# A two-layer decoder trunk in fp32 on one core: the MLPs' weights are prepared in a new order, five plain pairs instead of four, and plain tiles take their low halves from accumulating transfers

## The chip, the core and the metric

The kernel runs on one core of a Trainium2 chip. The metric is device time in microseconds (us); the engines are TensorE (PE; its weight loads are listed apart as PEld), VectorE (DVE), ScalarE (ACT), GpSimd (POOL) and SyncE (SP). SP and POOL only issue transfers here, apart from a few set-up instructions.

## The reference

One sequence of 512 tokens, width 1024, two layers. Each layer adds a mixer (layer 0: causal pooling and a convolution module; layer 1: latent attention with 16 heads), a cross-attention into 256 memory tokens, and a gated MLP with a causal convolution of three taps on the gate. A final RMSNorm follows. Everything is fp32.

```python
def conv_ffn(h, w_up, conv_w, conv_b, w_down):          # D_FF = 2816
    a, g = jnp.split(h @ w_up, 2, axis=-1)
    g = causal_dwconv(g, conv_w) + conv_b
    return (jax.nn.silu(g) * a) @ w_down

for l in range(DEPTH):                                   # DEPTH = 2
    x = x + (pool_conv_mixer if l % 2 == 0 else mla_attention)(rmsnorm(x, norm_mix_g[l]), ...)
    x = x + memory_cross_attention(rmsnorm(x, norm_xa_g[l]), rmsnorm(mem, norm_mem_g[l]), ...)
    x = x + conv_ffn(rmsnorm(x, norm_ffn_g[l]), ffn_w_up[l], ffn_conv_w[l], ffn_conv_b[l], ffn_w_down[l])
return rmsnorm(x, final_norm_g)
```

## The kernel before

**Number format.** Activations lie transposed: 128 channels by 512 tokens (`T`). Each operand of a matmul is split into a high half (a cast) and a low half (the rest), and a product is three matmuls, high by high, high by low, low by high (`mm3`, lines 173 to 175). Activations are split by an ACT cast and a DVE subtraction (lines 212 and 213). Weights come as tiles of 128 by 1024 (`wr`, one SP transfer of 512 KB, line 150, four buffers) and are split by `load_w` in the same way (lines 167 and 168) into `wh` and `wl`, three buffers each. `low_by_dma` (lines 160 and 161) makes the low half without DVE: ACT writes −1 times the tile, and a POOL transfer adds the tile from memory to it.

**The MLP** (`ffn`) works on 22 pairs of column blocks, a gate tile and an other tile, 128 columns each.

- The first four pairs (`PLAIN_PAIRS`) are *plain*: for each of the two tiles eight `mm3` of 512 columns into one PSUM bank `lin`, with weights from `load_w`. DVE multiplies the result by the row scale `rb`, `convolved` makes the gate `c` on ACT and DVE, and the product is split into `fh` and `fl`.
- Meanwhile `Operands.fill` builds the operands of the other 18 pairs on DVE and ACT, `OPERAND_STEPS` steps per plain tile: names `b…` and `t…`, from scaled activations `u`.
- The other 18 pairs are *paired*: a bilinear scheme forms both tiles by seven products (`a11`, `s1`, `s2`, `a12`, `s3`, `s4`, `a22`) of four `mm3` of 256 columns, in three banks `xyz`. `q` and `e` are copies of partial results; the bank of `a11` is used again by `s2`, so `q` must be copied first (line 684). The weight operands of the seven products come from four pieces per pair, `Weights.piece(0)` to `piece(3)`: the gate tile (split by `low_by_dma` into two buffers `wh1`, `wl1` of its own), the first sums, the second sums, and half of the other tile (the last three split by ACT and DVE, lines 559 and 560, in `wh` and `wl`). `need` releases pieces from a list by numbers, with `LEAD = 2`.
- `down()` is a generator that puts one `mm3` of 512 columns of the down projection behind each of the seven products. Its weights are tiles `dr` of 128 by 512 (256 KB, SP, line 638), one for each of eight output blocks and each of four groups of four pairs, split into `dwh` and `dwl`; the tile after the present one is fetched and split when the present one has done its first `mm3`. The fifth group (six pairs) follows as plain products, or in the last layer in `finale` (bank `fin`, weight halves `dh` and `dl`, lines 735 and 736).

**What sets the order.** A scheduler places the instructions of each engine in program order, moved forward by `tc.high_priority(offset=…)` (`AHEAD = 40` in `load_w`). Each engine then works its queue strictly in order, and so do the two queues that issue transfers, SP and POOL. A pool of 55 slots of 128 by 512 (`slot`) holds nearly all intermediate tiles, `dr` and the halves of activations among them.

In the latent attention, `kv` (the cross-attention's keys and values, kept in memory) is fetched and split by `split_kept` after the last head, and then follow the output projection and the cross-attention.

Of the kernel before, what the change touches and what calls it, by code (L numbers as in the profile page):

```python
# [19 lines left out]
P = 128  # L20
T = 512
# [39 lines left out]
RB_K = 6  # L61
LATE = (1, 4, 1, 3, 1, 4, 1)
FFN_GROUPS = (4, 4, 4, 4, 6)
PLAIN_PAIRS = 4
OPERAND_STEPS = 5
LEAD = 2
HALF = T // 2
KH = KD // 2

# [36 lines left out]
def kernel(ctx: ExitStack, tc: tile.TileContext, a):  # L106
# [46 lines left out]
    def parts():  # L153
        hi = wp.tile([P, WCOLS], F32R, tag="wh", name=uid("wh"), bufs=3)
        lo = wp.tile([P, WCOLS], F32R, tag="wl", name=uid("wl"), bufs=3)
        return hi, lo

    def low_by_dma(lo, raw, src):
# [232 lines left out]
        sp.dma_start(t, d)  # L391
        return t

    def split_kept(kv):
        kt, vt = kv
        return ([split_sb(fetch(t), "k", (P, 2, MEM)) for t in kt],
                [[split_sb(fetch(t), "v") for t in row] for row in vt])

    def split_kv(kv):
        kt, vt = kv  # L400
# [142 lines left out]
    class Weights:  # L543
# [16 lines left out]
            vec.tensor_tensor(lo[:, :n], raw, f(hi[:, :n]), ALU.subtract)  # L560
            self.put(names, hi, lo)

        def piece(self, n):
            if n == 0:
                self.g = load_raw(self.src[0], D)
                hi = wp.tile([P, WCOLS], F32R, tag="wh1", name=uid("wh1"), bufs=2)
                lo = wp.tile([P, WCOLS], F32R, tag="wl1", name=uid("wl1"), bufs=2)
                act.copy(hi, self.g)
                low_by_dma(lo, self.g, self.src[0])
                self.put(("a11", "a12"), hi, lo)  # L570
                return
            if n == 3:
                self.split(("a22",), self.r[:, T:])
                return
            s = wp.tile([P, WCOLS], F32, tag="ws", name=uid("ws"), bufs=2)
            if n == 1:
                self.r = load_raw(self.src[1], D)
                self.s2 = s[:, T:]
                vec.tensor_tensor(s[:, :T], self.r[:, :T], self.r[:, T:], ALU.add)
                vec.tensor_tensor(s[:, T:], s[:, :T], self.g[:, :T], ALU.add)  # L580
                self.split(("s1", "s2"), s)
            else:
                vec.tensor_tensor(s[:, :T], self.r[:, :T], self.g[:, :T], ALU.add)
                vec.tensor_tensor(s[:, T:], self.s2, self.g[:, T:], ALU.add)
                self.split(("s3", "s4"), s)


    SEVEN = (("a11", "b11", 0, 0), ("s1", "nt1", 1, 1), ("s2", "nt2", 1, 0), ("a12", "b21", 0, 2),
             ("s3", "t3", 2, 0), ("s4", "b22", 2, 1), ("a22", "t4", 3, 0))

    def ffn(layer, norm, nxt, extra=None):
        prod = []
        ahead = [linear(a["ffn_up"][layer, KF], norm.h)]
        norm.rate()
        ahead.append(linear(a["ffn_up"][layer, 0], norm.h))
        rb = norm.wide()
        ops = Operands(norm, rb)
        filling = ops.fill()

        def fill(n):  # L600
            for _ in range(n):
                next(filling, None)

        def w(i, j):
            return col("ffn_conv_w", (layer * 3 + j) * KF + i)

        def convolved(i, g):
# [4 lines left out]
            act.activation(c, c, AF.Silu)  # L612
            return c

        def plain(i):

            ps = ahead.pop(0) if ahead else linear(a["ffn_up"][layer, KF + i], norm.h)
# [5 lines left out]
            ps = ahead.pop(0) if ahead else linear(a["ffn_up"][layer, i], norm.h)  # L623
            if i:
                fill(OPERAND_STEPS)
            vec.tensor_tensor(g, ps, rb, ALU.mult)
            vec.tensor_tensor(c, c, g, ALU.mult)
            prod.append(split_sb(c, "f"))

        starts = [sum(FFN_GROUPS[:n]) for n in range(len(FFN_GROUPS) + 1)]  # L630

        def down():

            todo = [(n, m) for n in range(len(FFN_GROUPS) - 1) for m in range(KD)]

            def fetch_w(n, m):
                raw = slot("dr")
                sp.dma_start(raw, a["ffn_down"][layer, m][:, starts[n] * P:starts[n + 1] * P])
                return split_sb(raw, "dw")

            nextw = fetch_w(*todo[0])
            for j, (n, m) in enumerate(todo):
                hi, lo = nextw
                ps = bank("down")
                for k in range(KH):
                    c = slice(k * P, (k + 1) * P)
                    xh, xl = prod[starts[n] + k]
                    mm3(ps, hi[:, c], lo[:, c], xh, xl, k == 0, k == KH - 1)
                    if k == 0 and j + 1 < len(todo):
                        nextw = fetch_w(*todo[j + 1])  # L650
                    if k == KH - 1:
                        vec.tensor_tensor(x[m], x[m], ps, ALU.add)
                    yield

        todo = []

        def need(j):
            while len(todo) and todo[0][0] <= j:
                _, wt, n = todo.pop(0)
                wt.piece(n)  # L660

        pairs = {i: Weights(layer, i) for i in range(PLAIN_PAIRS, KF)}
        for i in pairs:
            todo.extend(((i - PLAIN_PAIRS) * 4 + n - 4 * (n == 0), pairs[i], n) for n in range(4))
        todo.sort(key=lambda t: t[0])
        lower = down()

        def paired(i):
            wt = pairs[i]
            base = (i - PLAIN_PAIRS) * 4  # L670
# [5 lines left out]
            for name, other, n, b in SEVEN:  # L676
                need(base + n + (LEAD if n else 0))
                hi, lo = wt.v[name]
                for k in range(KH):
                    s = slice(k * P, (k + 1) * P)  # L680
                    mm3(ps[b], hi[:, s], lo[:, s], *ops.v[other][k], b not in seen and k == 0, k == KH - 1, b in seen)
                seen.add(b)
                if name == "a11":
                    act.copy(q[:, :HALF], ps[0])  # L684
                elif name == "s1":
                    act.mul(e[:, :HALF], ps[1], -1.0)
                elif name == "s2":
                    act.copy(q[:, HALF:], ps[0])
# [12 lines left out]

        for i in range(PLAIN_PAIRS):
            if i == PLAIN_PAIRS - 1:
                need(LEAD)
# [390 lines left out]
    def latent_attention(norm, nxt, cs, sn, kv):  # L1095
# [302 lines left out]
```

## Time and profile before

| | |
|---|---|
| median of three runs | 1451.36 us (1450.86 to 1454.81) |
| profiled execution | 1447.31 us, its span 1445.5 us |
| mean granted TensorE clock | 0.978 |
| busy share of PE, DVE, ACT, POOL | 95%, 72%, 51%, 3% |
| `wr` loads of the MLPs (SP) | 88 of 512 KB, 3.5 us to landing |
| accumulating transfers (POOL) | 36 of 512 KB, 5.5 us to landing |
| `dr` loads (SP) | 64 of 256 KB, 4.9 us to landing |
| plain pairs of layer 0 and 1, to | 393.6 us, 1103.1 us |
| paired pairs of layer 0 and 1, to | 693.5 us, 1396.7 us |

Times in rows of the profile are us from the start of the span unless ns are meant (the mean of one in groups of instructions). In rows of the timeline the bracket at the end says how long the engine had stood before the instruction and which instruction released it. The granted clock is 1.00 or 0.50 at any moment, so a mean of 0.86 is a stretch with 28% at half speed. A `x2` row holds two instructions. A line number is that of the kernel before.

### The profile page before, as it was taken

How to read it: one execution, taken by the hardware profiler on the slowest of the kernel's cores; microseconds unless marked ns; L12 is line 12 of the kernel's file. 1: busy time of each engine (PE TensorE's matmuls, PEld its weight loads, DVE VectorE, ACT ScalarE, POOL GpSimd, SP SyncE). 2: the span in 40 equal slices, each digit the busy share in tenths (PEclk: the TensorE clock that was granted, in tenths of full speed). 3: DMA queues.
4: the chain of work that ended last, by engine and by line, in shares of the span. 5: the costliest groups of instructions: out<-in, count | busy, mean ns of one | idle time of the engine just before them, and what ended most of it. 6: DMA issues, size and time to landing. Idle time of an engine off the chain costs nothing.

```text
span 1445.5 us, 20372 instructions
## 1 busy us (share of the span) xinstructions
PE 1376.7 (95%) x7828; PEld 1184.6 (82%) x7828; DVE 1045.7 (72%) x1931; ACT 739.0 (51%) x1256; POOL 37.0 (3%) x53
## 2 busy tenths in 40 slices
PE   8999999999799999999999999999997999999997
PEld 6888878888588989898887777788876988989887
DVE  6999997556966767675869774754677767767665
ACT  6416466444444545454447775543454545545443
POOL 0000000000000000000000000000000000000000
PEclk9999999999889999999999999999997999999999
DMA  9335633124144545452321111421332445454421
GB/s 325 96 114 195 200 103 118 59 73 117 58 125 109 153 117 120 121 147 73 96 95 48 41 62 42 160 64 54 100 97 87 119 123 153 117 124 127 108 87 59
DMA packets 54673, 158.58 MB, mean 110 GB/s; under 512 B 6192, under 2 KB 7856, under 8 KB 54576
## 3 DMA queue, kind: packets, MB, share of 16 engines
q1 hardware_dynamic: 47664, 135.55, 28.4%
q0 software_dynamic: 5184, 18.88, 8.0%
q10 hardware_dynamic: 1728, 2.86, 0.5%
q8 instruction: 61, 1.00, 0.3%
q14 instruction: 36, 0.29, 0.1%
HBM read 153.06 MB, written 4.19 MB: 109 GB/s over the span
## 4 chain that ended last, share of the span: by engine, by line
PE 75%; DVE 11%; DMA 6%; ACT 4%; issue 2%; SPq 0%; DVEq 0%; ACTq 0%
PE lin L175 10%; PE lin L174 10%; PE lin L173 10%; PE xyz L173 6%; PE xyz L174 6%; PE xyz L175 6%; DMA dr<-in_ffn_down 5%; PE down L173 3%; PE down L174 3%; PE down L175 3%; PE kx L356 2%; DVE wl L560 2%; PE s L1222 1%; PE mpv L1259 1%; DVE wl L168 1%
## 5 line engine op out<-in xcount | busy, mean ns | idle before, releaser
L173 PE MATMUL xyz<-th,wh 128*128 128x256 f32 x864 | 249.8, 290 | 12.5 <-ACT q L684 10.4
L174 PE MATMUL xyz<-tl,wh 128*128 128x256 f32 x864 | 247.9, 288 | 0.0
L175 PE MATMUL xyz<-th,wl 128*128 128x256 f32 x864 | 245.8, 288 | 0.0
L167 ACT CAST wh<-wr 128x1024 fp32r<-128x1024 f32 (+2 forms) x136 | 129.5, 956 | 200.2 <-issue 90.0
L173 PEld LDWEIGHTS xyz<-th,wh 128*128 128x128 f32 x864 | 169.1, 196 | 25.6 <-ACT q L684 13.2
L168 DVE TENSOR_TENSOR wl<-wr,wh 128x1024 fp32r<-128x1024 f32 (+2 forms) x136 | 149.8, 1103 | 52.2 <-ACT wh L167 50.4
L174 PEld LDWEIGHTS xyz<-tl,wh 128*128 128x128 f32 x864 | 169.3, 196 | 7.4
L173 PE MATMUL lin<-hh,wh 128*128 128x512 f32 x400 | 160.5, 401 | 13.0 <-ACT wh L167 7.1
L175 PEld LDWEIGHTS xyz<-th,wl 128*128 128x128 f32 x864 | 168.0, 196 | 0.0
L175 PE MATMUL lin<-hh,wl 128*128 128x512 f32 x400 | 158.7, 397 | 5.1 <-DVE wl L168 5.1
L174 PE MATMUL lin<-hl,wh 128*128 128x512 f32 x400 | 159.2, 398 | 2.1 <-DVE hl L281 2.1
L560 DVE TENSOR_TENSOR wl<-ws,wh 128x1024 fp32r<-128x1024 f32 x72 | 88.1, 1224 | 96.4 <-ACT wh L559 96.4
L559 ACT CAST wh<-ws 128x1024 fp32r<-128x1024 f32 x72 | 75.5, 1048 | 127.9 <-PE xyz L174 127.2
L173 PE MATMUL down<-fh,dwh 128*128 128x512 f32 x256 | 105.4, 412 | 24.4 <-ACT dwh L212 24.4
L174 PE MATMUL down<-fl,dwh 128*128 128x512 f32 x256 | 103.0, 402 | 0.0
L175 PE MATMUL down<-fh,dwl 128*128 128x512 f32 x256 | 101.9, 398 | 0.0
L173 PEld LDWEIGHTS lin<-hh,wh 128*128 128x128 f32 x400 | 76.8, 192 | 30.0 <-ACT wh L167 8.8
L175 PEld LDWEIGHTS lin<-hh,wl 128*128 128x128 f32 x400 | 76.5, 191 | 22.2 <-DVE wl L168 6.7
L174 PEld LDWEIGHTS lin<-hl,wh 128*128 128x128 f32 x400 | 76.5, 191 | 21.4 <-DVE hl L281 6.6
L883 DVE SCALAR_TENSOR_TENSOR cv<-a,con,cv 128x509 f32<-128x509 f32 (+25 forms) x115 | 79.8, 733 | 0.1
L173 PEld LDWEIGHTS down<-fh,dwh 128*128 128x128 f32 x256 | 49.9, 195 | 30.1 <-ACT dwh L212 27.9
L213 DVE TENSOR_TENSOR dwl<-dr,dwh 128x512 fp32r<-128x512 f32 x64 | 43.9, 686 | 30.8 <-ACT dwh L212 30.8
(403 smaller groups left out, 3105.9 us busy)
## 6 DMA issues: line engine op xcount, KB each, us to landing
wr<-in_ffn_up SPq DMA_DIRECT2D x88, 512.0 KB, 3.5
wl<-in_ffn_up POOLq DMA_DIRECT2D x36, 512.0 KB, 5.5
dr<-in_ffn_down SPq DMA_DIRECT2D x64, 256.0 KB, 4.9
wr<-in_xa_wk SPq DMA_DIRECT2D x16, 512.0 KB, 3.5
wr<-in_xa_wv SPq DMA_DIRECT2D x16, 512.0 KB, 4.3
wr<-in_xa_wq SPq DMA_DIRECT2D x16, 512.0 KB, 3.5
wr<-in_xa_wo SPq DMA_DIRECT2D x16, 512.0 KB, 3.4
wr<-in_ffn_down SPq DMA_DIRECT2D x16, 384.0 KB, 3.3
```

Source lines behind the costliest of these rows:

```text
L167: act.copy(hi[:, :n], raw[:, :n])
L168: vec.tensor_tensor(lo[:, :n], raw[:, :n], f(hi[:, :n]), ALU.subtract)
L173: pe.matmul(ps, ah, bh, start=first, stop=False, skip_group_check=more)
L174: pe.matmul(ps, ah, bl, start=False, stop=False, skip_group_check=more)
L175: pe.matmul(ps, al, bh, start=False, stop=last, skip_group_check=more)
L213: vec.tensor_tensor(l, src, f(h), ALU.subtract)
L356: pe.matmul(ps[:, j, :], w[:, k * P:(k + 1) * P], mg[k], start=k == 0, stop=k == KD - 1)
L559: act.copy(hi[:, :n], raw)
L560: vec.tensor_tensor(lo[:, :n], raw, f(hi[:, :n]), ALU.subtract)
L883: vec.scalar_tensor_tensor(cv[i][:, s:], gl[i][:, :T - s], w, cv[i][:, s:], ALU.mult, ALU.add)
L1222: pe.matmul(ps[i], q[:, i * P:(i + 1) * P], k[:, :P * (i + 1)], start=True, stop=True)
L1259: pe.matmul(ps[e * VH:(e + 1) * VH, j * P:], w, turned[n][j], start=j == 0, stop=j == TB - 1)
```

## The change

`PLAIN_PAIRS` goes from 4 to 5 and `OPERAND_STEPS` from 5 to 4.

The weights of plain tiles no longer come from `load_w`: `run_plain(t)` issues the load of tile t + 4 and the split of tile t + 3, and the split is `act.copy` and `low_by_dma`. The halves lie in five buffers, the two of `wh1`, `wl1` and the three of `wh`, `wl`, by the tile's number modulo 5. The first tiles are issued with priority offsets of 150 and 40. Accumulating transfers go from 36 to 54 in the program.

`Weights.piece` becomes six methods, and `NEXT` and `ENTER` say at which product, or before which plain tile, each is called and for which later pair. `down()` fetches `dr` two tiles ahead and splits it one ahead. The kept keys and values are fetched when the last head's scores have been issued (`fetch_kept`), and split where both was done before.

```diff
-PLAIN_PAIRS = 4
-OPERAND_STEPS = 5
-LEAD = 2
+PLAIN_PAIRS = 5
+OPERAND_STEPS = 4
+EARLY = 150
...
+    def early_parts():
+        hi = wp.tile([P, WCOLS], F32R, tag="wh1", name=uid("wh1"), bufs=2)
+        lo = wp.tile([P, WCOLS], F32R, tag="wl1", name=uid("wl1"), bufs=2)
         return hi, lo
...
-    def split_kept(kv):
+    def fetch_kept(kv):
         kt, vt = kv
-        return ([split_sb(fetch(t), "k", (P, 2, MEM)) for t in kt],
-                [[split_sb(fetch(t), "v") for t in row] for row in vt])
+        return [fetch(t) for t in kt], [[fetch(t) for t in row] for row in vt]
...
-        def piece(self, n):
...
+        def load_gate(self):
+            self.g = load_raw(self.src[0], D)
+        def load_other(self):
+            self.r = load_raw(self.src[1], D)
+        def gate(self):
+            hi, lo = early_parts()
+            act.copy(hi, self.g)
+            low_by_dma(lo, self.g, self.src[0])
+            self.put(("a11", "a12"), hi, lo)
+        def first_sums(self):
...
+        def second_sums(self):
...
+        def other(self):
+            self.split(("a22",), self.r[:, T:])
...
+    NEXT = {"a11": ((0, "second_sums"),), "s1": ((0, "other"), (2, "load_gate")), "s2": ((1, "load_other"),),
+            "s3": ((1, "first_sums"),), "s4": ((2, "gate"),)}
+    ENTER = {-4: ((0, "load_gate"),), -3: ((0, "gate"), (0, "load_other"), (1, "load_gate")),
+             -2: ((1, "gate"),), -1: ((0, "first_sums"),)}
 
     def ffn(layer, norm, nxt, extra=None):
         prod = []
-        ahead = [linear(a["ffn_up"][layer, KF], norm.h)]
+        plain_raw, plain_w = {}, {}
+        tiles = 2 * PLAIN_PAIRS
+        def load_plain(t):
+            if t < tiles:
+                plain_raw[t] = load_raw(weights_of(t), D)
+        def split_plain(t):
+            if t < tiles:
+                raw = plain_raw.pop(t)
+                hi, lo = (early_parts if t % 5 < 2 else parts)()
+                act.copy(hi, raw)
+                low_by_dma(lo, raw, weights_of(t))
+                plain_w[t] = hi, lo
+        def run_plain(t):
+            load_plain(t + 4)
+            split_plain(t + 3)
+            for p, what in ENTER.get(t - tiles, ()):
+                getattr(pairs[PLAIN_PAIRS + p], what)()
+            hi, lo = plain_w.pop(t)
...
+        with tc.high_priority(offset=EARLY):
+            for t in range(2):
+                load_plain(t)
+                split_plain(t)
+        with tc.high_priority(offset=AHEAD):
+            load_plain(2)
+            split_plain(2)
+            load_plain(3)
+        ahead = [run_plain(0)]
...
-            nextw = fetch_w(*todo[0])
+            fetch_w(0)
+            fetch_w(1)
+            nextw = split_sb(raw.pop(0), "dw")
...
                     if k == 0 and j + 1 < len(todo):
-                        nextw = fetch_w(*todo[j + 1])
+                        nextw = split_sb(raw.pop(j + 1), "dw")
+                        fetch_w(j + 2)
...
-                need(base + n + (LEAD if n else 0))
+                for p, what in NEXT.get(name, ()):
+                    if i + p < KF:
+                        getattr(pairs[i + p], what)()
...
         for n in range(HEADS + LAG + 1):
+            if n == HEADS:
+                kv = fetch_kept(kv)
...
-        kv = split_kept(kv)
+        kv = split_kv(kv)
```

Where the instructions stand. Rows give line, operation, output and inputs (the numbers in the names count tiles) and the shape; lines of the changed kernel are its own.

DVE in layer 0's plain stage, before, around the last plain gate tile but one. `g687` is the scaled gate, `wl719` and `wl732` are low halves of plain weights, `tl…`, `bl…` and `u…`, `ta…`, `tb…` belong to the operands.

```order
L621 TENSOR_TENSOR g687_3309<-lin677_3262,rb646_3142 128x512
L168 TENSOR_TENSOR wl719_3403<-wr717_3400,wh718_3402 128x1024
L610 SCALAR_TENSOR_TENSOR c688_3311<-g687_3309,con_72,c688_3311 128x511
L213 TENSOR_TENSOR tl694_3348<-tb682_3296,th693_3347 128x512
L611 SCALAR_TENSOR_TENSOR c688_3311<-g687_3309,con_72,c688_3311 128x510
L510 SCALAR_TENSOR_TENSOR u695_3351<-x2_75,con_72,rb646_3142 128x512
L510 SCALAR_TENSOR_TENSOR u696_3353<-x6_79,con_72,rb646_3142 128x512
```

The same place on DVE after, at the last gate tile but one (`g717`); `wl743` is the low half of the first paired pair's first sums.

```order
L679 TENSOR_TENSOR g717_3430<-lin710_3393,rb656_3167 128x512
L534 TENSOR_TENSOR ta715_3426<-tb716_3427,u711_3418 128x256
L535 TENSOR_TENSOR tb716_3427<-ta715_3426,u712_3420 128x256
L668 SCALAR_TENSOR_TENSOR c718_3432<-g717_3430,con_72,c718_3432 128x511
L219 TENSOR_TENSOR tl725_3474<-u712_3420,th724_3473 128x512
L669 SCALAR_TENSOR_TENSOR c718_3432<-g717_3430,con_72,c718_3432 128x510
L565 TENSOR_TENSOR wl743_3542<-ws741_3538,wh742_3541 128x1024
```

No subtraction for a plain tile's weights is left on DVE; the operands' steps and the paired pairs' pieces remain.

SP in layer 0's paired stretch, before. `dr828` and `dr843` are tiles 6 and 7 of the first group.

```order
L150 DMA wr846_4112<-in_ffn_up 128x1024
L150 DMA wr851_4157<-in_ffn_up 128x1024
L638 DMA dr814_3919<-in_ffn_down 128x512
L150 DMA wr871_4276<-in_ffn_up 128x1024
L150 DMA wr880_4328<-in_ffn_up 128x1024
L638 DMA dr828_4017<-in_ffn_down 128x512
L638 DMA dr843_4106<-in_ffn_down 128x512
```

SP after, at the same place; here `dr831` is tile 6 of the first group.

```order
L150 DMA wr826_3972<-in_ffn_up 128x1024
L150 DMA wr827_3991<-in_ffn_up 128x1024
L698 DMA dr801_3825<-in_ffn_down 128x512
L698 DMA dr812_3916<-in_ffn_down 128x512
L150 DMA wr855_4143<-in_ffn_up 128x1024
L150 DMA wr856_4161<-in_ffn_up 128x1024
L698 DMA dr831_4014<-in_ffn_down 128x512
```

The loads still come as two `wr` and then one or two `dr`, but a `dr` is now that of a tile further on.

ACT at the step from the last plain tile to the first paired pair, before. `wh757` is cast into the buffer that the last plain tile used, `c728` and `fh738` belong to the last plain pair, `th…` are operands, `q747` copies the bank of the first product.

```order
L559 CAST wh757_3547<-wr710_3384 128x512
L212 CAST th736_3494<-u733_3484 128x512
L612 ACTIVATE c728_3448<-c728_3448 128x512
L212 CAST fh738_3500<-c728_3448 128x512
L535 ACTIVATE th740_3504<-ta734_3488 128x512
L212 CAST th742_3508<-tb735_3489 128x512
L684 COPY q747_3515<-xyz744_3512 128x256
```

ACT after, at the same step (`wh770`, `c740`, `fh751` and `q756` are the counterparts).

```order
L564 CAST wh770_3634<-wr721_3442 128x512
L667 ACTIVATE c740_3533<-g739_3531,con_72 128x512
L218 CAST th745_3572<-u736_3523 128x512
L540 ACTIVATE th747_3576<-ta737_3527 128x512
L670 ACTIVATE c740_3533<-c740_3533 128x512
L218 CAST th749_3580<-tb738_3528 128x512
L218 CAST fh751_3586<-c740_3533 128x512
L737 COPY q756_3593<-xyz753_3590 128x256
```

The same kinds of rows stand between the cast and `q`; the first step of `c` comes behind the cast and the two operand rows ahead of `fh`.

More of the change, by code (lines that the diff above doesn't have):

```diff
@@ L155, in parts @@
         lo = wp.tile([P, WCOLS], F32R, tag="wl", name=uid("wl"), bufs=3)
+        return hi, lo
+    def early_parts():
+        hi = wp.tile([P, WCOLS], F32R, tag="wh1", name=uid("wh1"), bufs=2)
+        lo = wp.tile([P, WCOLS], F32R, tag="wl1", name=uid("wl1"), bufs=2)
         return hi, lo
@@ L561, in split @@
             self.put(names, hi, lo)
-        def piece(self, n):
[L564 to L585, printed above, removed]
@@ L588, with sums @@
-    SEVEN = (("a11", "b11", 0, 0), ("s1", "nt1", 1, 1), ("s2", "nt2", 1, 0), ("a12", "b21", 0, 2),
-             ("s3", "t3", 2, 0), ("s4", "b22", 2, 1), ("a22", "t4", 3, 0))
+        def sums(self):
+            return wp.tile([P, WCOLS], F32, tag="ws", name=uid("ws"), bufs=2)
+        def load_gate(self):
[7 more added lines that the diff above has]
+            self.put(("a11", "a12"), hi, lo)
@@ new lines, in first_sums @@
+        def first_sums(self):
+            s = self.sums()
+            self.s2 = s[:, T:]
+            vec.tensor_tensor(s[:, :T], self.r[:, :T], self.r[:, T:], ALU.add)
+            vec.tensor_tensor(s[:, T:], s[:, :T], self.g[:, :T], ALU.add)
+            self.split(("s1", "s2"), s)
+        def second_sums(self):
+            s = self.sums()
+            vec.tensor_tensor(s[:, :T], self.r[:, :T], self.g[:, :T], ALU.add)
+            vec.tensor_tensor(s[:, T:], self.s2, self.g[:, T:], ALU.add)
+            self.split(("s3", "s4"), s)
@@ new lines, in other @@
+        def other(self):
+            self.split(("a22",), self.r[:, T:])
+    SEVEN = (("a11", "b11", 0), ("s1", "nt1", 1), ("s2", "nt2", 0), ("a12", "b21", 2),
+             ("s3", "t3", 0), ("s4", "b22", 1), ("a22", "t4", 0))
+    NEXT = {"a11": ((0, "second_sums"),), "s1": ((0, "other"), (2, "load_gate")), "s2": ((1, "load_other"),),
+            "s3": ((1, "first_sums"),), "s4": ((2, "gate"),)}
+    ENTER = {-4: ((0, "load_gate"),), -3: ((0, "gate"), (0, "load_other"), (1, "load_gate")),
+             -2: ((1, "gate"),), -1: ((0, "first_sums"),)}
@@ L591, in ffn, with weights_of @@
     def ffn(layer, norm, nxt, extra=None):
         prod = []
-        ahead = [linear(a["ffn_up"][layer, KF], norm.h)]
+        plain_raw, plain_w = {}, {}
+        tiles = 2 * PLAIN_PAIRS
+        def weights_of(t):
+            return a["ffn_up"][layer, t // 2 + (0 if t % 2 else KF)]
+        def load_plain(t):
[8 more added lines that the diff above has]
+                plain_w[t] = hi, lo
@@ new lines, in run_plain @@
+        def run_plain(t):
[4 more added lines that the diff above has]
+            hi, lo = plain_w.pop(t)
+            ps = bank("lin")
+            for k in range(KD):
+                c = slice(k * P, (k + 1) * P)
+                mm3(ps, hi[:, c], lo[:, c], *norm.h[k], k == 0, k == KD - 1)
+            return ps
+        pairs = {i: Weights(layer, i) for i in range(PLAIN_PAIRS, KF)}
@@ L594, in ffn @@
+        with tc.high_priority(offset=EARLY):
[7 more added lines that the diff above has]
+        ahead = [run_plain(0)]
         norm.rate()
-        ahead.append(linear(a["ffn_up"][layer, 0], norm.h))
+        ahead.append(run_plain(1))
         rb = norm.wide()
@@ L615, in plain @@
         def plain(i):
-            ps = ahead.pop(0) if ahead else linear(a["ffn_up"][layer, KF + i], norm.h)
+            ps = ahead.pop(0) if ahead else run_plain(2 * i)
             if i:
@@ L622, in plain @@
             c = convolved(i, g)
-            ps = ahead.pop(0) if ahead else linear(a["ffn_up"][layer, i], norm.h)
+            ps = ahead.pop(0) if ahead else run_plain(2 * i + 1)
             if i:
@@ L634, in down, with fetch_w @@
             todo = [(n, m) for n in range(len(FFN_GROUPS) - 1) for m in range(KD)]
[L636 to L639, printed above, removed]
-            nextw = fetch_w(*todo[0])
+            def fetch_w(j):
+                if j < len(todo):
+                    n, m = todo[j]
+                    raw[j] = slot("dr")
+                    sp.dma_start(raw[j], a["ffn_down"][layer, m][:, starts[n] * P:starts[n + 1] * P])
+            raw = {}
+            fetch_w(0)
+            fetch_w(1)
+            nextw = split_sb(raw.pop(0), "dw")
             for j, (n, m) in enumerate(todo):
@@ L653, in down @@
                     yield
[L655 to L665, printed above, removed]
         lower = down()
@@ L669, in paired @@
             wt = pairs[i]
-            base = (i - PLAIN_PAIRS) * 4
             ps = [bank("xyz", (P, HALF)) for _ in range(3)]
@@ L675, in paired @@
             c = None
-            for name, other, n, b in SEVEN:
-                need(base + n + (LEAD if n else 0))
+            for name, other, b in SEVEN:
+                for p, what in NEXT.get(name, ()):
+                    if i + p < KF:
+                        getattr(pairs[i + p], what)()
                 hi, lo = wt.v[name]
@@ L702, in ffn @@
         for i in range(PLAIN_PAIRS):
-            if i == PLAIN_PAIRS - 1:
-                need(LEAD)
             plain(i)
```

## The prediction

> **What bounds the kernel now.** I read the page's first part, then PE's waits in order of time, then stretches of even work beside stretches with waits, and last the engines that end those waits.
>
> ```profile
> PE 1376.7 (95%) x7828; PEld 1184.6 (82%) x7828; DVE 1045.7 (72%) x1931; ACT 739.0 (51%) x1256; POOL 37.0 (3%) x53
> 303.00:338.50 35.50, 35.50 (x158) 29.02 (x157) 22.83 (x29) 15.85 (x22) 0.00 (x0) 1.00 0.31 101
> 660.00:690.00 30.00, 30.00 (x214) 28.07 (x213) 21.18 (x36) 12.48 (x21) 0.00 (x0) 1.00 0.26 79
> ```
>
> TensorE bounds, but its 95% hides slow clock and waits. The last two rows (columns: busy time of PE, PE's weight loads, DVE, ACT, POOL; granted clock; DMA share; GB/s) are stretches without a wait at clock 1.00. Two instructions of each count reach over an edge, so a 512-column matmul costs 35.50 / 156 = 0.228 us, and one of the pairs' mix (84 of 256 columns to 21 of 512) 30.00 / 212 = 0.1415; solved for the small one, 0.120. Elapsed time less count times price is what a stretch loses:
>
> ```profile
> 370.00:394.00 24.00, 17.99 (x73) 13.67 (x71) 22.35 (x40) 11.42 (x19) 0.00 (x0) 0.86 0.20 66
> 394.00:408.00 14.00, 8.26 (x35) 7.33 (x35) 9.03 (x17) 5.33 (x11) 0.00 (x0) 0.63 0.39 132
> 408.00:695.00 287.00, 273.15 (x1851) 252.96 (x1850) 198.92 (x321) 144.47 (x221) 14.63 (x18) 0.97 0.45 117
> 1080.00:1103.50 23.50, 17.50 (x71) 13.46 (x69) 21.41 (x38) 11.37 (x19) 0.00 (x0) 0.85 0.21 68
> 1103.50:1117.50 14.00, 8.15 (x34) 7.28 (x34) 8.77 (x17) 5.07 (x11) 0.00 (x0) 0.63 0.40 131
> 1117.50:1398.50 281.00, 269.52 (x1853) 249.67 (x1851) 197.14 (x319) 142.85 (x218) 13.82 (x16) 0.99 0.45 118
> 370.00:394.00 24.00, 16.79 (x61) 12.05 (x59) 2.05 (x3) 0.00 (x0) 0.86 0.20 66
> 1080.00:1103.50 23.50, 16.27 (x59) 11.82 (x57) 2.05 (x3) 0.00 (x0) 0.85 0.21 68
> ```
>
> The last two rows are those of the plain tiles alone (no POOL column): 61 and 59 of the 73 and 71 matmuls have 512 columns. So the plain stages lose 24.00 − 61 × 0.228 − 12 × 0.120 = 8.7 us and 8.6 us. The junctions to the first paired pair lose 14.00 − 35 × 0.1415 = 9.0 and 9.2. The paired stretches lose 287.00 − 1851 × 0.1415 = 25.1 and 281.00 − 1853 × 0.1415 = 18.8, together 43.9. That is 80 us in the MLPs, of which the change touches 61.
>
> What ends the waits in the plain stage:
>
> ```profile
> 375.73 0.79 PE L173 MATMUL lin<-hh,wh 128*128 128x512 f32 x1 [2.90 <-ACT wh L167]
> 379.15 0.79 PE L175 MATMUL lin<-hh,wl 128*128 128x512 f32 x1 [2.20 <-DVE wl L168]
> 386.89 0.50 PE L173 MATMUL lin<-hh,wh 128*128 128x512 f32 x1 [0.91 <-ACT wh L167]
> ```
>
> The weights' halves, made one tile ahead: the subtraction stands in a DVE queue that was busy 22.35 of 24.00 us (row 370 above).
>
> In the paired stretch it is the halves of a down-projection tile, and their wait is a DMA's:
>
> ```profile
> PE down L173 <- ACT dwh L212: 24.4, 16, 3.2
> ACT dwh L212 <- DMA dr<-in_ffn_down: 17.3, 16, 3.0
> 449.01 2.19 SPq L150 DMA_DIRECT2D wr<-in_ffn_up  x2
> 451.25 0.90 SPq L638 DMA_DIRECT2D dr<-in_ffn_down  x2
> 456.00 0.62 ACT L212 CAST dwh<-dr 128x512 fp32r<-128x512 f32 x1 [0.68 <-DMA dr<-in_ffn_down]
> 456.68 0.50 PE L173 MATMUL down<-fh,dwh 128*128 128x512 f32 x1 [2.32 <-ACT dwh L212]
> 457.50:460.90 3.40, 3.40 (x17) 3.21 (x16) 0.42 (x1) 0.63 (x3) 0.86 (x1) 0.50 0.44 53
> ```
>
> (Wait rows: who, for whom, us in all, times, longest.) The `dr` transfers stand in SP's queue behind two `wr` loads that wait for a buffer; they leave at 451.25, land before 456.00, and TensorE has stood 2.32 us. The next 3.40 us then run at clock 0.50. [...]
>
> **The change part by part.**
>
> *Plain tiles.* Each tile's weights are now cast three tiles ahead, and the low half is an ACT multiply and an accumulating transfer. DVE loses 8 subtractions of 1.10 us (L168 below) per layer, ACT gains 10 multiplies per layer (each about a cast, 0.96), POOL 9 more issues per layer.
>
> ```profile
> L167 ACT CAST wh<-wr 128x1024 fp32r<-128x1024 f32 (+2 forms) x136 | 129.5, 956 | 200.2 <-issue 90.0 <-PE lin L174 66.0 <-PE vx L175 17.5
> L168 DVE TENSOR_TENSOR wl<-wr,wh 128x1024 fp32r<-128x1024 f32 (+2 forms) x136 | 149.8, 1103 | 52.2 <-ACT wh L167 50.4 <-PE st L235 1.4 <-DMA kv<-kv 0.3
> L161 POOL DMA_DIRECT2D wl<-in_ffn_up x36: 862/862/1011, 347.8 to 1358.5; - x36
> DMA to landing us min/median/max: 5.2/5.5/7.5
> wr<-in_ffn_up SPq DMA_DIRECT2D x88, 512.0 KB, 3.5
> ```
>
> A tile lasts 24 × 0.228 = 5.46 us. With five buffers a cast may start when the tile five earlier ended, four tiles (21.8 us) before its own. Cast 0.96, multiply 0.96, issue 0.86, landing 5.5: 8.3 us, slack 13.5; at the longest landing, 11.5. The raw load (3.5 us) is issued a tile before its cast. So the 17.3 us go, clock included. Ends: 17.3, and 9 if in each layer one wait like the 2.90 and the slow clock behind it stay (8.7 us each, half of that kept). I take 17.3, since the slack is longer than any landing in the trace. DVE stays nearly full: the operand steps and a fifth pair's multiplies, counted in the changed order with the durations of these rows, come to 38 to 41 us of the 42.5 us from the row scale to the last plain tile. But it no longer feeds the plain tiles; its lateness shows at the junction. On POOL only such issues follow one another, each behind its multiply. On SP a `wr` load waits for a raw buffer of four, which the multiply frees; behind it stand the next `wr` and the first `dr`, needed 20 us later.
>
> *One more plain pair per layer.* 48 × 0.228 = 10.92 us instead of 84 × 0.120 = 10.08: 2 × 0.84 = 1.7 us lost.
>
> *Junction.*
>
> ```profile
> 399.24 0.58 PE L173 MATMUL xyz<-th,wh 128*128 128x256 f32 x1 [5.20 <-ACT q L684]
> 393.43 0.62 ACT L559 CAST wh<-wr 128x512 fp32r<-128x512 f32 x1 [0.81 <-PE lin L174]
> 394.51 0.63 ACT L612 ACTIVATE c<-c 128x512 f32<-128x512 f32 x1
> 397.26 0.62 ACT L212 CAST fh<-c 128x512 fp32r<-128x512 f32 x1 [2.12 <-DVE c L627]
> 398.82 0.36 ACT L684 COPY q<-xyz 128x256 f32<-128x256 f32 x1
> 402.71 0.79 PE L173 MATMUL down<-fh,dwh 128*128 128x512 f32 x1 [0.55 <-ACT dwh L212]
> 1112.32 0.80 PE L173 MATMUL down<-fh,dwh 128*128 128x512 f32 x1 [0.68 <-ACT dwh L212]
> L173 PE MATMUL xyz<-th,wh 128*128 128x256 f32 x864 | 249.8, 290 | 12.5 <-ACT q L684 10.4 <-ACT q L688 2.0
> ```
>
> The third product needs the bank that `q` empties, and ACT has ahead of `q` a cast that waits for the last plain tile, the SiLU, and `fh`, which waits for DVE. After the change the same rows stand there in nearly the same order. From the cast to the end of `q` is 399.18 − 393.43 = 5.75 us, covered by 12 × 0.120 = 1.44 of first product; about 5 us of idle and its slow clock remain, and no other work covers it, since every later product needs operands or banks of the same chain. Cost 0; ends 5 us more per layer (`c` comes from DVE, which may be some four of its 1.1 us subtractions behind) and 9 less (closed).
>
> *Paired pieces.* The sums, casts and transfers of a pair are the same instructions, placed by product; only whose need comes first moves. What pays is `dr` two tiles ahead: a tile lasts four products of 12 × 0.120 and four triples of 3 × 0.228, or 8.5 us. SP still has two `wr` ahead of two `dr`, but now a `dr` is due 8.5 us later than before, while it was late by 3.2 at the most. What is queued behind SP's waiting `wr` is thus again `dr`, with over 5 us left. Gone: 24.4, less 0.55 and 0.68 at the junctions (rows 402.71 and 1112.32), is 23.2 idle; half clock is 0.03 × 287 + 0.01 × 281 = 11.4. Another 2.0 us wait on the `q` of line 688 (last row above) and stay; some 7 us are attributed to nothing, of which I take half. Sum 23.2 + 11.4 + 3.4 = 38. Ends: 19 (half of the stalls come back as others) and 44. POOL's issues per pair are as before. ACT and DVE have 18 of 30 and 9 of 30 us free (row 660), which covers the pieces' new order. A raw tile more is live in the 55 slots.
>
> *Ends of the stages.*
>
> ```profile
> L173 PE MATMUL fin<-fh,dh 128*128 128x256 f32 x96 | 27.4, 286 | 1.4 <-ACT dh L735 1.4
> L175 PE MATMUL fin<-fh,dl 128*128 128x256 f32 x96 | 27.3, 284 | 0.3 <-DVE dl L736 0.3
> L174 PE MATMUL lin<-hl,wh 128*128 128x512 f32 x400 | 159.2, 398 | 2.1 <-DVE hl L281 2.1
> ```
>
> With seven products fewer, 9 down triples follow the last pair instead of 2: 6.2 us of work over the 1.7 us that the final projection waits. Gain 1.7 (ends 0, 1.7). The kept keys' DMAs go out before the last heads, and their splits find data: they stood ahead of the normed halves after the latent attention. Gain up to 2.1; I take it, with 0 as the other end. On SP eight such loads now pass one load of the attention's output weights and delay it by 8 issues of 0.45 us (0.90 for two `dr` above), 3.6 us of the 16 that three tiles of raw lead give it.
>
> Sum: 17.3 + 38 + 1.7 + 2.1 − 1.7 = 57.4. The profiled execution took 1447.31 (span 1445.5), 4.05 under the median of the runs: 1389.9 for such an execution, 1394 for the median.
>
> **Rivals.**
>
> *Half the paired stalls remain,* as pieces that arrive late or because the slots run out (51 of 55 are in use at the peak before, counted from allocation and release in the order). 1394 + 19 = 1413. For: the two `dr` are still behind two `wr`. Against: 8.5 us more lead.
>
> *All of them remain,* only the plain stage gains: 1394 + 38 = 1432.
>
> *The junction takes the DVE backlog:* 5 us a layer, 1404. For: DVE near 90% over the plain stage. *Or it closes:* 18.2 us more, 1376. Against: ACT's order.
>
> *The clock doesn't follow the stalls.* If the 0.50 has another cause, half clock stays: 11.4 in the pairs and 24 × 0.14 + 23.5 × 0.15 = 6.9 in the plain stages, 1394 + 18 = 1412. [...] Against: the row of 457.50, straight behind a stall, and 1.00 where there is none.
>
> *Slower: accumulating transfers served one after the other, at a late pace.* Those in the trace are never closer than 6 us (below); in the plain stage they come every 5.46. If each took S us alone, 14 tiles (7 a layer; three are made ahead) would run at S. It decides at 14 × (S − 5.46) > 57, S over 9.6 us; at 12 us, 92 lost, 1485.
>
> ```profile
> 347.80 1.01 POOL L161 DMA_DIRECT2D wl<-in_ffn_up  x1 [229.68 <-ACT wl L160]
> 354.20 0.87 POOL L161 DMA_DIRECT2D wl<-in_ffn_up  x1 [5.39 <-ACT wl L160]
> ```
>
> Against: two at 6.4 us, and no landing over 7.5 with DVE busy at 72% beside them. [...]
>
> *No effect,* SP's and the pieces' order deciding all: 1451.
>
> **Chances.** Main case 0.62; junction later 0.08; half of the stalls 0.10; clock stays 0.05; all stay 0.05; junction closes 0.05; slower 0.03; none 0.02. The range 1380 to 1422 leaves out the last four. Faster by over 0.3% (4.4 us, about what a measurement of this kernel tells from no change) 0.95, within 0.02, slower 0.03.
>
> **What would show it.** Plain stages: no `lin` wait of over 1 us, clock 1.00, tiles of 5.5 us. Paired stretches: the row of `down` for `dwh` under 5 us, clock 1.00 throughout. Junction: again some 5 us for `q`. The final projection without wait; `lin` for `hl` near zero. Wrong if the accumulating landings pass 10 us, if `dr` is again the last to come, or if `xyz` waits for the pieces.

## The result, and the profile after

The changed kernel takes 1384.04 us (median of three, 1383.12 to 1384.61) against 1451.36: a ratio of 0.9529, 95% interval 0.9505 to 0.9553, or 67 us less. Its profiled execution took 1383.12 us with a span of 1381.3, 64.2 less than the span before. In two of the runs below one execution each took 1943.34 and 1914.49 us at a mean granted clock of 0.653 and 0.655; the medians count it, the ratios don't.

The first line of the page, and then stretches of the MLPs (layer 0, then layer 1; plain stage, first 14 us of the pairs, the other pairs). Columns: busy time of PE, PE's weight loads, DVE, ACT, POOL; granted clock; DMA share; GB/s.

```profile
PE 1352.6 (98%) x7756; PEld 1168.1 (85%) x7756; DVE 1020.0 (74%) x1897; ACT 748.8 (54%) x1264; POOL 52.9 (4%) x71
340.50:394.80 54.30, 54.30 (x246) 44.95 (x244) 42.02 (x82) 33.79 (x47) 6.92 (x8) 1.00 0.74 154
394.80:408.80 14.00, 8.58 (x46) 7.87 (x45) 10.17 (x19) 6.91 (x13) 0.00 (x0) 0.76 0.44 151
408.80:655.00 246.20, 246.20 (x1738) 230.18 (x1737) 186.33 (x300) 134.18 (x206) 13.80 (x17) 1.00 0.49 128
1012.00:1066.70 54.70, 54.70 (x247) 45.29 (x246) 42.34 (x83) 34.17 (x48) 6.92 (x8) 1.00 0.74 154
1066.70:1080.70 14.00, 8.80 (x45) 8.14 (x44) 9.99 (x18) 6.84 (x13) 0.00 (x0) 0.76 0.44 150
1080.70:1327.00 246.30, 246.30 (x1739) 230.25 (x1738) 184.82 (x298) 132.99 (x205) 12.97 (x15) 1.00 0.49 127
```

The plain stages run at clock 1.00 without a wait, and so do the pairs: 246.20 − 1738 × 0.1415 = 0.3 us lost, where the stretches before lost 25.1 and 18.8. The stalls left in the MLPs are one at the junction of each layer and a new one at the end of layer 1. First PE's waits for `q` (in all, times, longest), then the first of them; then the end of layer 1, ACT and PE:

```profile
PE xyz L179 <- ACT q L737: 10.6, 2, 5.4
401.69 0.58 PE L179 MATMUL xyz<-th,wh 128*128 128x256 f32 x1 [5.42 <-ACT q L737]
1330.23 1.75 ACT L786 CAST dh<-wr 128x384 fp32r<-128x384 f32 x4
1331.89 0.61 ACT L218 CAST dwh<-dr 128x512 fp32r<-128x512 f32 x1
1332.55 0.50 PE L179 MATMUL down<-fh,dwh 128*128 128x512 f32 x1 [1.16 <-ACT dwh L218]
1334.18 0.50 PE L181 MATMUL down<-fh,dwl 128*128 128x512 f32 x1 [0.54 <-DVE dwl L219]
```

The `dr` transfers still leave late, in the same place behind two `wr` loads, but now nobody waits for them. SP's issues and the splits of `dr`:

```profile
448.46 2.19 SPq L150 DMA_DIRECT2D wr<-in_ffn_up  x2
450.70 0.42 SPq L698 DMA_DIRECT2D dr<-in_ffn_down  x1
451.58 0.61 ACT L218 CAST dwh<-dr 128x512 fp32r<-128x512 f32 x1
457.33 0.61 ACT L218 CAST dwh<-dr 128x512 fp32r<-128x512 f32 x1
```

The cast at 451.58 takes a tile that was fetched earlier; the one that left at 450.70 comes later. Accumulating transfers are 54 now (their times to landing below), and the slowest took longer than any before, 10.2 us against 7.5. It isn't alone: the 24 that go out shortly before and during the plain stages landed in a median of 7.7 us, the other 30 in 5.4.

```profile
DMA to landing us min/median/max: 5.3/5.7/10.2
```

### The profile page after: what moved, and what is told of

Read it like the earlier page. It is cut to its first block, busy times and chain, and to the rows that moved or that the text cites. A ratio compares the mean times of both kernels' runs of the same rounds, so it can differ in the third digit from the quotient of the medians.

```text
span 1381.3 us, 20270 instructions
## 1 busy us (share of the span) xinstructions
PE 1352.6 (98%) x7756; PEld 1168.1 (85%) x7756; DVE 1020.0 (74%) x1897; ACT 748.8 (54%) x1264; POOL 52.9 (4%) x71
## 4 chain that ended last, share of the span: by engine, by line
PE 88%; DVE 8%; ACT 2%; issue 1%; DMA 0%; SPq 0%; DVEq 0%; ACTq 0%
PE lin L179 11%; PE lin L181 11%; PE lin L180 11%; PE xyz L179 8%; PE xyz L180 8%; PE xyz L181 8%; PE down L180 4%; PE down L179 4%; PE down L181 4%; DVE cv L934 3%; PE s L1273 1%; PE mpv L1310 1%; DVE wl L174 1%; PE t L1298 1%; PE vx L180 1%
## 5 line engine op out<-in xcount | busy, mean ns | idle before, releaser
L179 PE MATMUL xyz<-th,wh 128*128 128x256 f32 x816 | 230.8, 284 | 10.6 <-ACT q L737 10.6
L181 PE MATMUL xyz<-th,wl 128*128 128x256 f32 x816 | 231.5, 284 | 0.0
L180 PE MATMUL xyz<-tl,wh 128*128 128x256 f32 x816 | 231.3, 284 | 0.0
L173 ACT CAST wh<-wr 128x1024 fp32r<-128x1024 f32 (+3 forms) x120 | 112.7, 944 | 161.8 <-issue 60.6
L179 PEld LDWEIGHTS xyz<-th,wh 128*128 128x128 f32 x816 | 155.7, 192 | 23.2 <-ACT q L737 14.9
L180 PEld LDWEIGHTS xyz<-tl,wh 128*128 128x128 f32 x816 | 156.8, 192 | 7.1
L174 DVE TENSOR_TENSOR wl<-wr,wh 128x1024 fp32r<-128x1024 f32 (+3 forms) x120 | 130.1, 1086 | 42.4 <-ACT wh L173 40.9
L181 PEld LDWEIGHTS xyz<-th,wl 128*128 128x128 f32 x816 | 156.7, 192 | 0.0
L167 POOL DMA_DIRECT2D wl<-in_ffn_up x54 | 46.9, 868 | 1058.2 <-ACT wl L166 1058.2
L670 ACT ACTIVATE c<-c 128x512 f32<-128x512 f32 x44 | 27.8, 632 | 58.5 <-DVE c L669 58.3
```

The costliest lines, as they stand in the source:

```text
L167: pool.dma_start(lo, src, accum_op=ALU.add)
L173: act.copy(hi[:, :n], raw[:, :n])
L174: vec.tensor_tensor(lo[:, :n], raw[:, :n], f(hi[:, :n]), ALU.subtract)
L179: pe.matmul(ps, ah, bh, start=first, stop=False, skip_group_check=more)
L180: pe.matmul(ps, ah, bl, start=False, stop=False, skip_group_check=more)
L181: pe.matmul(ps, al, bh, start=False, stop=last, skip_group_check=more)
```

## The experiments

Unless told otherwise a run starts from the changed kernel. "Loss" is elapsed time less matmuls at the prices of the prediction. Five runs were executed once only; as executions of one kernel differ (1384.44 to 1387.96 us in one of the runs, 1442.59 to 1453.68 for the kernel before beside it), those are read from their traces.

### Down-projection tiles fetched two ahead, alone

From the kernel before:

```diff
-                        nextw = fetch_w(*todo[j + 1])
+                        nextw = split_sb(raw.pop(j + 1), "dw")
+                        fetch_w(j + 2)
```

> The kernel before, with one part of the change alone: each tile of the down projection is fetched two tiles ahead instead of one and still split one ahead. If the paired stalls were the late dr transfers (my account), PE's wait of down for dwh falls from 24.4 us to under 4, the slow clock behind those waits goes, and the time is about 1451 - 40 = 1411. If SP's queue was blocked by the order in which the weight pieces ask for their buffers (rival: the new table of pieces is what helped), at least half of the waits stay and the time is 1430 or more.

Measured: 1407.69 us, ratio to before 0.9707 (0.9691 to 0.9723). The paired stretches of both layers:

```profile
408.00:670.00 262.00, 262.00 (x1846) 244.79 (x1846) 197.73 (x317) 143.19 (x219) 14.63 (x18) 1.00 0.48 127
1094.00:1356.00 262.00, 262.00 (x1846) 244.76 (x1845) 196.07 (x316) 141.64 (x217) 13.81 (x16) 1.00 0.48 125
```

No wait of `down` is left but those at the two junctions, the clock is 1.00, and the loss is 262.00 − 1846 × 0.1415 = 0.8 us. With the pieces in their old places, this part alone cures the pairs, 43 us.

### The same part undone

```diff
-                        nextw = split_sb(raw.pop(j + 1), "dw")
-                        fetch_w(j + 2)
+                        nextw = fetch_w(*todo[j + 1])
```

> The changed kernel with this part undone: down-projection tiles are fetched and split one ahead as before, all else as changed. My account: the waits come back, about 1384 + 40 = 1424. Rival (the pieces' new places suffice): 1384 to 1395, down waits for dwh under 5 us.

Measured: 1432.9 us, 0.9874 (0.9855 to 0.9892), 49 more than the changed kernel. PE's waits:

```profile
PE down L179 <- ACT dwh L218: 29.8, 16, 5.2
```

Before it was 24.4 us in as many waits. The longest, 5.2 us, comes after the last pair of layer 1; the others sum to 24.6, where the pairs of the kernel before waited 23.2. So the new table of pieces does nothing for the pairs, and the rival falls in both directions. The extra wait at the end is why the part is worth 49 us here and 43 alone.

### Plain tiles: subtractions, three buffers, and the place of the sums

Besides the fifth pair and the operand steps, four things changed together in the plain stage: accumulating transfers, five buffers, weights asked for three tiles ahead, and the paired sums placed later. The first run takes back the transfers:

```diff
-                low_by_dma(lo, raw, weights_of(t))
+                vec.tensor_tensor(lo, raw, f(hi), ALU.subtract)
```

> The changed kernel with the plain tiles' low halves made by a VectorE subtraction, still three tiles ahead in five buffers; no multiply on ScalarE and no accumulating transfer for plain tiles. If the lead alone cured the plain stage: 1384, plain stages still without waits, the junction the same. If taking work from VectorE was needed: 10 subtractions of 1.1 us per layer on an engine that is busy 42 of 54.3 us there and nearly full from the first operand on; they come out either as lin waits or at the junction, 5 to 11 us a layer, 1394 to 1406.

Measured: 1385.01 us, 0.9554 (0.9537 to 0.9570). The plain stage, its second half and the junction:

```profile
340.50:394.80 54.30, 54.30 (x245) 44.96 (x244) 46.70 (x85) 27.73 (x40) 1.88 (x2) 1.00 0.33 88
370.00:394.00 24.00, 24.00 (x107) 19.89 (x106) 24.00 (x43) 13.74 (x20) 1.88 (x2) 1.00 0.41 88
394.80:408.80 14.00, 7.55 (x43) 6.87 (x42) 11.45 (x21) 6.63 (x13) 0.00 (x0) 0.76 0.41 138
```

DVE is busy 24.00 of 24 us and TensorE never waits for it. A full VectorE by itself therefore doesn't stall the plain stage; the junction waits 6.39 instead of 5.42 us, and no other wait in the MLPs is longer. Then only the three old buffers, with transfers and with subtractions:

```diff
-                hi, lo = (early_parts if t % 5 < 2 else parts)()
+                hi, lo = parts()
```

> The changed kernel with plain tiles in three buffers (wh, wl) instead of five; low halves by accumulating transfer. A cast then starts when the tile three earlier ended, two tiles (10.9 us) before its own, against a chain of 8.3 us: if only the chain counts, no lin wait and 1384. At the last tiles the paired pair's first sums ask for the same three buffers. If five buffers were needed, lin waits of 1 to 3 us come back in the last four tiles, 1388 to 1400.

> The changed kernel with plain tiles in three buffers and VectorE subtractions: what is left of the change in the plain stage is the order, that is, casts that go out as soon as a buffer is free and the paired sums one tile before the end. In the kernel before, ACT cast the sums of two pairs ahead of the last two plain tiles, and the second of them waited for VectorE. If that place was the cause: no lin wait, 1385 like the run with subtractions in five buffers. If five buffers or the accumulating transfers are needed besides: waits of 2 to 3 us as before, 1395 to 1405.

Measured, one run each: 1387.20 and 1388.25 us. With transfers, `lin` waits 0.33 and 1.22 us in layer 0 and 0.62 and 0.24 in layer 1, each time for a transfer; with subtractions not at all (its 4 us more lie at the junctions, with waits of 5.62 and 0.62 us in layer 0 and 10.2 us of slow clock in each layer). The second run's plain stage toward its end:

```profile
370.00:395.00 25.00, 25.00 (x112) 20.71 (x111) 25.00 (x44) 15.45 (x23) 1.88 (x2) 1.00 0.49 117
```

So the transfers need the five buffers to go without waits, and neither is needed for the plain stage's gain. With three buffers a cast has 10.9 us; the transfers of that plain stage landed in a median of 7.8 us, which with 0.96, 0.96 and 0.86 for cast, multiply and issue makes 10.6. What is left is the order. In the kernel before, ACT cast two paired sums ahead of the last plain tile but one, and the second of them waited for VectorE (first row). TensorE waited 2.90 us for that tile's cast (row 375.73 of the prediction). The last tile's cast waited for a buffer (third row):

```profile
373.16 1.05 ACT L559 CAST wh<-ws 128x1024 fp32r<-128x1024 f32 x1 [0.37 <-DVE ws L584]
374.63 1.04 ACT L167 CAST wh<-wr 128x1024 fp32r<-128x1024 f32 x1
385.79 1.04 ACT L167 CAST wh<-wr 128x1024 fp32r<-128x1024 f32 x1 [3.68 <-PE lin L174]
```

The next run has three buffers and subtractions, asks for the weights one tile ahead, and has the sums where they were; the second sums of the first paired pair are not made again at `a11`:

```diff
+    ENTER = {-3: ((0, "load_gate"), (0, "gate"), (1, "load_gate"), (1, "gate"), (0, "load_other"),
+                  (0, "first_sums"), (0, "second_sums"))}
...
         def run_plain(t):
-            load_plain(t + 4)
-            split_plain(t + 3)
             for p, what in ENTER.get(t - tiles, ()):
                 getattr(pairs[PLAIN_PAIRS + p], what)()
+            load_plain(t + 2)
+            split_plain(t + 1)
```

> The changed kernel, but its plain stage in the order of before: three buffers, VectorE subtractions, weights asked for one tile ahead, and the first paired pair's first and second sums ahead of the weights of the last two plain tiles, on ScalarE as in the kernel before. The run with three buffers and subtractions but without this order had no lin wait (plain stages 55.4 us). If the place of the sums caused the plain stage's waits: two waits of 2 to 3 us and one of about 1 come back in each layer with 6.8 us of slow clock, 16 to 18 us in all, about 1405. If the waits stay away, the cause is the fourth of eight tiles being under less VectorE work (four operand steps a tile instead of five), and the time is about 1388.

Measured, in one run: 1397.74 us. The same stretch, PE's longest wait there, and what ACT did ahead of it:

```profile
370.00:400.00 30.00, 22.12 (x86) 16.99 (x86) 28.03 (x49) 14.45 (x23) 0.87 (x1) 0.89 0.32 83
390.29 0.80 PE L179 MATMUL lin<-hh,wh 128*128 128x512 f32 x1 [6.69 <-ACT wh L626]
381.05 1.06 ACT L564 CAST wh<-ws 128x1024 fp32r<-128x1024 f32 x1 [0.64 <-DVE ws L587]
388.24 1.05 ACT L564 CAST wh<-ws 128x1024 fp32r<-128x1024 f32 x1
389.19 1.04 ACT L626 CAST wh<-wr 128x1024 fp32r<-128x1024 f32 x1
398.54 1.04 ACT L626 CAST wh<-wr 128x1024 fp32r<-128x1024 f32 x1 [1.96 <-PE lin L180]
```

The waits are back, 6.69, 0.24 and 0.95 us in layer 0, and the plain stages lose some 10.6 us each; less came back in all than expected, the junction below making up for some. The plain tile's cast (389.19) stands behind the casts of two paired sums (381.05, 388.24), which come from a DVE that works down a queue: that is most of the 6.69 us. Two of the three buffers belong to those sums from then on, so the last tile's cast (398.54) waits until TensorE has left the third: that is the 0.95 us. Four operand steps a tile, which this run keeps, are thus not what cured the stage.

Two things stay open. The kernel before waited 2.20 us more for the subtraction of the tile at 375.73; here that came back as 0.24, so the order of DVE's queue had a share in it that no run separates. And asking for the weights one tile ahead came together with the place of the sums. Up to the seventh tile it moves nothing: in layer 0 those casts come at the same times from the start of the stage, within 0.01 us, as in the run with three buffers, subtractions and three tiles ahead. For the last tiles it is what puts the sums first.

The junction waits only 2.6 us here. The reading, which no run tests, is that the stall gave DVE the time that it lacks there.

### Four plain pairs

```diff
-PLAIN_PAIRS = 5
-OPERAND_STEPS = 4
+PLAIN_PAIRS = 4
+OPERAND_STEPS = 5
```

> The changed kernel with four plain pairs and five operand steps as before. By the work alone 1.7 us less (0.84 a layer): 1382.3. If the fifth pair pays for itself as time in which VectorE finishes the operands: the junction's wait grows from 5.4 us by 1 to 4 us a layer and the time is 1384 to 1390.

Measured: 1400.31 us, 0.9651 (0.9616 to 0.9686): 16 us slower, where the count of work says 1.7 faster and the rival said 6 slower at most. The first 14 us of the pairs, and PE's waits:

```profile
383.80:397.80 14.00, 3.00 (x14) 2.09 (x13) 14.00 (x27) 7.09 (x13) 0.00 (x0) 0.71 0.37 81
PE xyz L179 <- ACT q L737: 12.6, 2, 6.3
PE xyz L179 <- ACT bh L524: 8.3, 2, 4.8
```

DVE is busy without a break and TensorE 3.00 of 14: the first product waits for operands (`bh`, in layer 0 also 1.13 us for an accumulating transfer) and a later one for `q`. Per layer 17.1 us of slow clock follow. The fifth pair is the time in which DVE finishes the operands.

### The junction loosened

The last plain pair's multiplies, convolution and split (`finish`) are issued after the second copy of `q` in the first paired pair:

```diff
-OPERAND_STEPS = 4
+OPERAND_STEPS = 5
...
+            if i == PLAIN_PAIRS - 1:
+                tail.append((pg, ps))
+                return
...
                     act.copy(q[:, HALF:], ps[0])
+                    if tail:
+                        finish()
```

> The changed kernel with the junction loosened: the last plain pair's multiplies, convolution and split are issued after the first paired pair's second q copy, and OPERAND_STEPS is 5, so that the operands are done a tile earlier. If the junction's 5 us wait is the queue ahead of q on ScalarE and VectorE (the last plain pair's own work, needed by nobody until the second down group), it falls to 1 to 2 us with no slow clock behind it: 5 to 7 us a layer less, 1371 to 1374. If VectorE's backlog holds the operands themselves, 3 us or more of wait stay and the time is 1378 to 1384.

Measured: 1372.84 us, 0.9462 (0.9448 to 0.9475). The stretch from the last plain tile on, and ACT:

```profile
395.10:409.10 14.00, 12.51 (x86) 11.24 (x85) 10.97 (x19) 8.01 (x13) 0.09 (x1) 1.00 0.45 152
395.04 0.63 ACT L564 CAST wh<-wr 128x512 fp32r<-128x512 f32 x1 [0.40 <-PE lin L180]
395.57 0.62 ACT L540 ACTIVATE th<-ta 128x512 fp32r<-128x512 f32 x1
396.10 0.60 ACT L218 CAST th<-tb 128x512 fp32r<-128x512 f32 x1
396.69 0.37 ACT L754 COPY q<-xyz 128x256 f32<-128x256 f32 x1
```

`q` is copied at 396.69, where the changed kernel had its matmul waiting until 401.69, and the clock stays at 1.00. The two edits together are worth 5.6 us a layer; they were not told apart, but the rows that are gone from ahead of `q` are the last plain pair's own, for which nobody was waiting.

### The final projection's weights behind the last `dwh`

From that run:

```diff
             last = finale(layer, k0, KF - k0)
+            for _ in range(2):
+                next(lower)
             next(last)
```

> The run with the late tail, and in the last layer the final projection's weights are cast after the last split of a down tile (two steps of down first). There the casts dh stood ahead of dwh on ScalarE, and down waited 1.16 and 0.54 us. If that order was the cause: 1.7 us less, 1371.1. If fin then waits for dh instead: within 0.5 us of 1372.8.

Measured: 1369.9 us, 0.9441 (0.9411 to 0.9470), the lowest median of all. Its trace has no wait of over 0.1 us from the last pair to the final projection, and its span (1367.9) is 3.2 shorter than that of the run it starts from. That is more than the 1.7 us of the waits; 0.5 is the junction's wait for `dwh`, 0.30 and 0.49 us where it had been 0.57 and 0.73, which the edit doesn't touch, and the last microsecond is not accounted for.

### The kept keys and values

> The changed kernel with the kept keys and values fetched where they were before, after the last head. My prediction gave this part 2.1 us (the wait of lin for hl). The two traces differ by 3.8 us from the attention's output projection to the cross-attention (40.9 against 37.1). If the part does it all: 3.8 us longer than the changed kernel, about 1388; if only the wait comes back, 2.1, about 1386.

(`fetch_kept` is called right ahead of `split_kv`.) Measured, in one run: 1384.31 us. Layer 1's plain stage starts at 1011.4, in the changed kernel at 1011.3: the place of the fetch does nothing. Then each tile fetched and split in turn, as before:

```diff
+        return ([split_sb(fetch(t), "k", (P, 2, MEM)) for t in kt],
+                [[split_sb(fetch(t), "v") for t in row] for row in vt])
```

> The changed kernel with the kept keys and values as before entirely: each tile fetched and split in turn after the last head. Fetching later alone changed nothing (span 1382.5 against 1381.3, plain stage of layer 1 starts at 1011.4 against 1011.3). If it was the interleaving of fetches and splits that cost, the waits of lin for hl come back (2.1 us) and the stretch is 3 to 4 us longer: about 1387. If neither, 1384, and the gain there comes from elsewhere.

Measured, in one run: 1387.48 us. `lin` waits again, 2.1 of these 2.4 us at the place where it did before:

```profile
L180 PE MATMUL lin<-hl,wh 128*128 128x512 f32 x432 | 170.0, 393 | 2.4 <-DVE hl L287 2.4
```

The plain stage of layer 1 starts at 1014.6, so some 3.3 us come from fetching all before the first split.

## Why the prediction held, and where its steps failed

It gave 1394 in a range of 1380 to 1422; 1384.04 is 10 us better than that. Of the 67.3 us, 64.2 are in the spans; the rest is that the profiled execution before lay 4.05 us under its median and the one after only 0.92. The parts below, 42.9, 17.3, 2 and 3.3 less 1.7, come to 63.8 of the 64.2.

- **Pairs: mechanism shown, size short.** 38 predicted; by the two traces 43.9 less about 1 in all, 42.9. The steps that were mis-sized are "some 7 us are attributed to nothing, of which I take half" and the 2.0 us for `q` that "stay": nearly all of both went with the stalls. Taking the part alone and undoing it settle the cause (43 and 49 us).
- **Plain stage: size right, cause wrong in the main.** 17.3 predicted and gained; that is the whole loss of the stage, which any full cure would give. The step "the weights' halves, made one tile ahead: the subtraction stands in a DVE queue that was busy" took DVE's load for the cause. With DVE busy 25.00 of 25 us, subtractions and three buffers the stage runs without a wait, as long as the paired sums don't stand ahead of the last plain casts. The five buffers and the transfers are not necessary; whether they would do with the sums in their old place, no run shows. The slack was smaller than 13.5 us, too: with landings of 7.7 us instead of 5.5 the chain of 8.3 us is some 10.5, and 11.3 of the 21.8 us are left. With five buffers that was enough, with three it was not.
- **One more plain pair: the step with the wrong sign.** "1.7 us lost" counted TensorE's work and left out what VectorE does meanwhile; without the fifth pair the kernel is 16 us slower. Neither the new order with four pairs (1400.31) nor the old order with five (1397.74, one run) comes near the two together (1384.04).
- **Junction: as predicted.** Wait 5.42 and 5.20 us for 5.20 and 5.17, `q` behind the same rows. The loss went from 9 to about 8 us a layer; the wait for `dwh` behind it (0.55 and 0.68) is gone, and of 10.2 us of slow clock 6.8 are left. Most of the case "junction closes" could be had, as the tail run shows: 5.6 us a layer of the 9.1 that it counted.
- **Final projection: gained nothing.** The step "6.2 us of work over the 1.7 us that the final projection waits" held for `fin`, but the order put its casts ahead of a `dwh`, and 1.16 and 0.54 us of wait came back there. What was late next was not named.
- **Kept keys: right in sign, wrong in cause.** 2.1 predicted for the earlier fetch; some 3.3 measured, for fetching all before splitting.
- **Rivals.** The accumulating transfers came closer than 6 us and the slowest took 10.2, over the bound that the prediction set for itself; the slack was larger, and no matmul waited for one. Why they land later there than in the pairs is not shown. VectorE is as busy in the plain stage (42.02 of 54.30 us) as in the pairs (186.33 of 246.20), so its load alone doesn't explain it; the DMA share is higher, 0.74 against 0.49. "The clock doesn't follow the stalls" fell: with the stalls the slow clock went; of ten stretches at 0.50 in the MLPs of the kernel before, the two at the junctions are left.

## What to carry over

When an engine waits, look at what stands ahead of the awaited instruction in its engine's queue, not at how busy that engine is. Here moving work that nobody needs yet behind work that somebody waits for was worth some 11 us (with one operand step more a tile), and taking ten subtractions a layer from VectorE about 1. The transfer that always came late in the same place was cured by asking for the next but one, as its buffer could be had. And a stage that costs TensorE a little more may pay as time for another engine to finish: leave it out once before calling it a cost.

## What the runs showed of the clock

In the trace of the kernel before, the ten stretches at 0.50 in the MLPs last 3.41, 6.83 or 10.24 us, that is one, two or three times 3.413 us, and their starts are whole multiples of 3.413 us apart (457.53, 522.38 and 587.24 us: 19 times each; 129.71 / 38 = 3.413). The two of the changed kernel, at 399.91 and 1072.34 us, last 6.83 us and are 197 times 3.413 us apart. Both traces were cut into steps of this length from these starts, from 300 us to the last 10. Of the 622 steps at 1.00, those in which TensorE was idle for up to 1.86 us were all followed by 1.00, and the twelve with 1.93 to 3.41 us idle all by 0.50. Of the 21 steps at 0.50, the twelve with up to 0.13 us idle were all followed by 1.00, and the nine with 0.55 to 3.15 us all by another at 0.50. Two pairs of neighbouring steps of the kernel before:

```profile
1164.00:1167.40 3.40, 1.62 (x9) 1.42 (x10) 1.12 (x2) 2.53 (x5) 0.42 (x1) 1.00 0.21 78
1167.50:1170.90 3.40, 3.40 (x28) 3.22 (x27) 1.13 (x1) 1.84 (x3) 0.35 (x1) 1.00 0.70 107
1355.20:1358.60 3.40, 1.47 (x9) 1.09 (x8) 0.78 (x2) 3.00 (x5) 0.08 (x1) 1.00 0.25 93
1358.60:1362.00 3.40, 3.40 (x16) 3.30 (x15) 0.34 (x1) 0.85 (x2) 0.78 (x1) 0.51 0.52 81
```

The wait of 2.34 us from 1163.44 on lies across two steps (0.64 and 1.69 us idle), 1.78 us of it in the first row, and the clock stayed at 1.00. The wait of 1.93 us in the third row lies inside one step, and the row behind it ran at 0.51. Half of such a slow step, 1.7 us, is an estimate of what it costs at most. In the run with the late fetch of the kept keys the waits of 1.16 and 0.55 us at the end, 1.71 us together, were followed by 0.50, although steps with 1.69 and 1.86 us idle were not in the kernel before. In the changed kernel the waits there (1.16 and 0.54 us) lie in two steps, with 0.36 and 1.35 us idle, and the clock stayed at 1.00. That run's slow stretch, and the stretch of the changed kernel:

```profile
1334.60:1338.00 3.40, 3.40 (x10) 2.62 (x9) 0.42 (x1) 0.00 (x0) 0.00 (x0) 0.50 0.79 220
1331.00:1337.00 6.00, 4.29 (x21) 3.17 (x20) 4.26 (x10) 2.33 (x6) 0.00 (x0) 1.00 0.55 140
```

The span of the run with the late fetch is 1.2 us longer. Why the clock goes to 0.50 behind some idle stretches and not behind others, no run shows.
